# Weight-block sums moved from POOL to DVE in a one-core convolution-and-FFN layer, with padded tile pools and a rewritten last half

## The chip, the cores and the metric

The kernel runs on one core of a Trainium2 chip. The metric is the device time of one execution in microseconds (us), the median over runs. TensorE is called PE, VectorE DVE, ScalarE ACT, GpSimd POOL and SyncE SP. The transfers are issued by SP and ACT.

## What is computed

The reference is one layer on 2048 tokens of width 1024, float32 in and out, batch 1, with depth 1 (so only the convolution mixer and the FFN):

```python
mod = c_act @ ada_w[i] + ada_b[i]
sh_m, sc_m, g_m, sh_f, sc_f, g_f = jnp.split(mod, N_ADA, axis=-1)
h = modulate(rms_norm(x, norm_gains[i, 0]), sh_m, sc_m)
h = short_conv_mixer(h, conv_w_in[j], conv_w[j], conv_w_out[j])
x = x + g_m[:, None, :] * rms_norm(h, norm_gains[i, 1])
h = modulate(rms_norm(x, norm_gains[i, 2]), sh_f, sc_f)
h = swiglu(h, ffn_w_gate_up[i], ffn_w_down[i])
x = x + g_f[:, None, :] * rms_norm(h, norm_gains[i, 3])
```

`short_conv_mixer` is a product to 3 x 1024 features (gate b, gate c, value), a gate, a causal convolution of 3 taps along the tokens, a second gate and a product back to 1024. `swiglu` has an inner width of 2816.

## The kernel before

**Tiling.** Tokens are taken in two units (0 and 1) of 1024, each of two halves of 512. The stages follow each other as in0, out0, in1, out1, gu0, down0, gu1, down1: the product into the mixer, the product out of it, gate and up, down, for each unit. Every stage is done as one level of the Strassen-Winograd scheme: a product of 2 x 2 blocks becomes seven products P1 to P7. Their feature operands are A11, A12, A22 and the sums S1 to S4, their weight operands the blocks 11, 12, 21, 22 and sums of them. Every operand is split in a high part (a cast on ACT) and a low part (a subtraction on DVE), and a product of 4 chunks takes 3 matmuls a chunk: 12 matmuls of 128 x 512 make a slot, the unit of the program's clock.

**Weights.** A group of weights (tiles like `in7b`, `gu11b`: four or five blocks of 128 x 512 in the ring of raw tiles) goes through steps that run a fixed number of slots ahead of its product: loads 9 slots ahead, sums of blocks 7, the high part (ACT, into a tile like `in7P`) 5, the low part (DVE, into the same tile) 4. `Blocks.sum` makes the sums in the stages in and gu: 12 becomes 22-12 ahead of P7 or P6 (called T3), 11+ becomes 12+11 ahead of P6, 21 becomes 21-11+ and 11+ becomes 22-11+ ahead of P5. All four are POOL's, but T3 of the first three groups of in0, which is DVE's. Other sums of weights stay as they are: those of `Between` (`gu0b` to `gu2b`, between the slots of in0 and in1) on DVE, and those that `sums_later` makes for out and down and keeps in DRAM (`out1b`, `down9b`), on POOL. POOL also adds the squares of the norms (`nq`, `out0q`, `down1q`), makes two of the sums of features in `sums`, and the powers of the norms.

**Order.** Every engine executes its instructions in the order in which the program writes them (the helper at L75 records all of them, so all rows of the trace are of that line). An instruction that waits holds up everything behind it on its engine. `Group.after` puts ACT copies of a bank after P1, P6 and P5 and DVE additions after the others; PE goes on adding in the same bank, so a later product waits for the ACT copy.

**The opening.** `start` writes the order of the first three groups of in0 by hand: norms, the modulation, the products of A11, S3, A12 and S2, with `advance("sums", ...)`, `advance("high", ...)` and `advance("low", ...)` between them.

**The end.** In down1 the last half of the tokens has eight tiles of 128 x 512. Each is squared on ACT and added to the sum of squares. `last_half` then takes the mean on PE (`lasts`), 1/sqrt (POOL's power `lastp`, DVE's `lastt` and `lastq`), spreads it on PE (`lastb`, from the diagonal `lastd`), and makes x + gate x norm x z for eight tiles: five on DVE (two instructions each, reading `lastb`), three on POOL (reading `lastr`, an ACT copy of it; their gate is put in before by ACT). `xl` are the tiles of x. The tiles of the half before (`xo`, scaled with `o10r`) are still being written while this runs: one every 2 slots.

Of the kernel before, what the change touches and what calls it, by code (L numbers as in the profile page):

```python
# [10 lines left out]
F32 = mybir.dt.float32  # L11
# [35 lines left out]
def hybrid_conv_layer(  # L47
# [34 lines left out]
    sb = ctx.enter_context(tc.tile_pool(name="sb", bufs=1))  # L82
# [3 lines left out]
    def big(name, dt=F32):  # L86
        return sb.tile([P, 4, CH], dt, tag="big", bufs=NBIG, name=name)

    def raw(name):
        return sb.tile([P, CH], F32, tag="raw", bufs=NRAW, name=name)  # L90

    def pair(name):
        return sb.tile([P, 2, CH], F32, tag="wp", bufs=NWP, name=name)
# [42 lines left out]
    vt = const.tile([P, 112], F32, name="vt")  # L136
# [164 lines left out]
    class Blocks:  # L301
# [194 lines left out]
    class Group:  # L496
# [119 lines left out]
        def ready_z(self, c):  # L616
# [183 lines left out]
    for s in slots:  # L800
# [5 lines left out]
        else:  # L806
            b = of.setdefault((ph.name, s.n), Blocks(ph.kind, s.grp, ph.name == "in0" and s.n < LEAD))
# [68 lines left out]
    def after_down(ph, tok):  # L876
# [10 lines left out]
        yield from spread_later(q, f"o{u}{tok}", partial(put, rb, 0))  # L887
# [16 lines left out]
        for k in range(KD):  # L904
# [6 lines left out]
            yield 2  # L911
# [4 lines left out]
    POOLS = (5, 6, 7)  # L916

    def last_half(ph):

        u, tok = ph.u, 1  # L920
        st = bank("lasts")
        for t in range(4):
            PE.matmul(st[:, t : t + 1], ph.acc[tok][:, t * P : (t + 1) * P], mean, start=True, stop=True)
# [5 lines left out]
        rb = sb.tile([P, CH], F32, tag="rb", bufs=NRB, name="lastr")  # L929
        A.copy(rb, b)  # L930
        mine = [k for k in range(KD) if k not in POOLS]
        for n in range(len(mine)):
            if n < len(POOLS):
                k = POOLS[n]
                z, xt = ph.z(tok, k), ph.xt[k]
                G.tensor_tensor(z, z, rb, ALU.mult)
                G.tensor_tensor(xt, xt, z, ALU.add)
            k = mine[n]
# [4 lines left out]
        for k in POOLS:  # L943
            SP.dma_start(out_tile(u, tok, k), ph.xt[k])
        yield

    def before_last(ph):
# [4 lines left out]
        yield 1  # L952
        for k in POOLS:
            z = ph.z(1, k)
            A.activation(z, z, AF.Copy, scale=col(mG[1], k))
# [271 lines left out]
    schedule(first["down1"] + 73, lambda: run(before_last(phases[-1])))  # L1227
# [85 lines left out]
```

## Time and profile before

| | us |
|---|---|
| median of 3 runs | 2040.47 |
| lowest and highest | 2039.4 and 2041.07 |
| the profiled execution | 2041.43 |
| its span in the trace | 2039.3 |
| PE busy | 1941.7 |
| DVE busy | 1444.0 |
| ACT busy | 855.2 |
| POOL busy | 691.1 |

The time of an execution is 2.1 us longer than the span between the first and the last instruction that the trace shows. Busy time is the sum over instructions of an engine; an engine that is not busy waits or has nothing to do.

### The profile page before, as it was taken

Reading aid. Unit: us, or ns where it says so; the run is one execution under the profiler, and the core shown is the slowest. Engines: PE = TensorE matmul, PEld = TensorE weight load, DVE = VectorE, ACT = ScalarE, POOL = GpSimd, SP = SyncE. Lnnn points to the kernel's source line nnn. Section 1 sums busy time; section 2 is a strip of 40 time slices with the busy share of each in tenths; the row PEclk is TensorE's granted clock in tenths of the full one; section 3 lists DMA queues with packets and bytes.
Section 4 is the critical chain, followed back from the end, with each engine's and each line's share of the span. In section 5 each row is a group of like instructions: output and inputs, shape, how many; then the busy total and the mean of one; then the engine's idle time right before and its main releaser. Section 6 shows DMA issues by size and latency. Waiting matters only on the chain.

```text
span 2039.3 us, 25010 instructions
## 1 busy us (share of the span) xinstructions
PE 1941.7 (95%) x8432; PEld 1578.8 (77%) x8432; DVE 1444.0 (71%) x1878; ACT 855.2 (42%) x1382; POOL 691.1 (34%) x451
## 2 busy tenths in 40 slices
PE   5799998999989899999999999999999999999995
PEld 2578886778767778887888888887888888888884
DVE  4887887886989685699767656667767455465465
ACT  5443355632333663343333445544333333344451
POOL 0324541301542133357856431111443343311022
PEclk9899999999999999999999999999999999999998
DMA  9259959879766875477656788567646234285544
GB/s 382 74 205 352 358 203 327 322 266 347 243 212 206 300 258 175 151 232 257 224 186 218 256 280 308 196 249 258 222 162 220 94 127 132 67 326 208 203 145 136
DMA packets 206193, 463.19 MB, mean 227 GB/s; under 512 B 23024, under 2 KB 38512, under 8 KB 199152
## 3 DMA queue, kind: packets, MB, share of 16 engines
q1 hardware_dynamic: 179136, 397.49, 56.9%
q10 hardware_dynamic: 26928, 64.10, 8.3%
q8 instruction: 66, 1.08, 0.2%
q14 instruction: 63, 0.52, 0.1%
HBM read 328.33 MB, written 133.17 MB: 226 GB/s over the span
## 4 chain that ended last, share of the span: by engine, by line
PE 70%; DVE 13%; DMA 8%; ACT 4%; issue 3%; POOL 1%; SPq 0%; ACTq 0%; DVEq 0%; POOLq 0%
PE gu1P L75 20%; PE gu0P L75 16%; PE down1P L75 10%; PE down0P L75 10%; PE in0P L75 6%; PE in1P L75 5%; PE out1P L75 2%; DMA xx<-xt_d 1%; PE out0P L75 1%; DVE ada L75 1%; DMA xr<-x_d 1%; DVE zz L75 1%; DMA kgu1P<-gu1P 1%; DVE in0y L75 1%; DMA x<-xx 1%
## 5 line engine op out<-in xcount | busy, mean ns | idle before, releaser
L75 DVE TENSOR_TENSOR gu1a<-gu1P,gu1a 128x512 f32<-128x512 f32 x63 | 43.4, 690 | 93.0 <-PE gu1P L75 86.2
L75 DVE TENSOR_TENSOR gu0a<-gu0P,gu0a 128x512 f32<-128x512 f32 x63 | 43.2, 687 | 59.5 <-PE gu0P L75 54.0
L75 POOL TENSOR_TENSOR down0q<-down0q,down0q 128x512 f32<-128x512 f32 x14 | 26.0, 1859 | 152.3 <-ACT down0q L75 152.2
L75 POOL TENSOR_TENSOR down1q<-down1q,down1q 128x512 f32<-128x512 f32 x10 | 16.2, 1618 | 147.0 <-ACT down1q L75 147.0
L75 DVE CUSTOM_DVE_ANT_0 ada<-ada,c 128x512 f32<-128x512 f32 x80 | 62.5, 791 | 0.2 <-ACT c L75 0.2
L75 ACT COPY gu1a<-gu1P 128x512 f32<-128x512 f32 x42 | 24.5, 587 | 89.7 <-PE gu1P L75 78.1
L75 ACT COPY gu0a<-gu0P 128x512 f32<-128x512 f32 x42 | 24.5, 584 | 73.4 <-PE gu0P L75 65.9
L75 ACT COPY gu1g<-gu1P 128x512 f32<-128x512 f32 x24 | 14.1, 588 | 90.7 <-PE gu1P L75 85.9
L75 POOL TENSOR_TENSOR gu1a<-gu1a 128x512 f32<-128x512 f32 x11 | 19.5, 1776 | 89.8 <-DVE gu1g21s L75 24.7
L75 DVE TENSOR_TENSOR gu1g<-gu1P,gu1g 128x512 f32<-128x512 f32 x24 | 16.6, 691 | 44.9 <-ACT gu1g L75 43.6
L75 POOL TENSOR_TENSOR nq<-nq,nq 128x512 f32<-128x512 f32 x28 | 45.7, 1630 | 3.0 <-ACT nq L75 2.8
L75 ACT COPY gu0g<-gu0P 128x512 f32<-128x512 f32 x24 | 14.1, 586 | 72.6 <-PE gu0P L75 72.6
L75 POOL TENSOR_TENSOR out1q<-out1q,out1q 128x512 f32<-128x512 f32 x14 | 24.2, 1726 | 58.5 <-ACT out1q L75 58.4
L75 DVE TENSOR_TENSOR xx<-xx,zz 128x512 f32<-128x512 f32 x32 | 35.9, 1121 | 5.4 <-DMA xx<-xt_d 4.4
L75 DVE TENSOR_TENSOR gu0g<-gu0P,gu0g 128x512 f32<-128x512 f32 x24 | 16.6, 690 | 31.8 <-ACT gu0g L75 31.3
L75 POOL TENSOR_TENSOR out0q<-out0q,out0q 128x512 f32<-128x512 f32 x14 | 24.7, 1764 | 42.4 <-ACT out0q L75 42.3
L75 POOL TENSOR_TENSOR in0b<-in0b,in0b 128x512 f32<-128x512 f32 x7 | 10.7, 1533 | 79.4 <-DVE in1y L75 37.3
L75 POOL TENSOR_TENSOR gu0a<-gu0a 128x512 f32<-128x512 f32 x11 | 19.5, 1777 | 48.3 <-DVE gu0g11s L75 8.0
L75 ACT ACTIVATE gu1a<-gu1a 128x512 f32<-128x512 f32 x42 | 26.5, 633 | 15.0 <-DVE xo L75 7.7
L75 ACT ACTIVATE nq<-xx 128x512 f32<-128x512 f32 x32 | 20.2, 631 | 28.9 <-DVE xx L75 24.7
L75 ACT ACTIVATE gu0a<-gu0a 128x512 f32<-128x512 f32 x42 | 26.6, 633 | 13.5 <-DVE gu0a L75 12.2
L75 DVE TENSOR_TENSOR down2P<-down2P,down2P 128x512 fp32r<-128x512 f32 x14 | 11.1, 795 | 28.6 <-ACT down2P L75 28.6
(3209 smaller groups left out, 7014.8 us busy)
## 6 DMA issues: line engine op xcount, KB each, us to landing
ada<-ada_d SPq DMA_DIRECT2D x64, 256.0 KB, 5.2
act0A<-gu0a SPq DMA_DIRECT2D x33, 256.0 KB, 4.1
act1A<-gu1a SPq DMA_DIRECT2D x33, 256.0 KB, 3.2
ada<-ada_d SPq DMA_DIRECT2D x16, 512.0 KB, 8.9
zz<-z SPq DMA_DIRECT2D x32, 256.0 KB, 4.2
xx<-xt_d SPq DMA_DIRECT2D x32, 256.0 KB, 4.4
x<-xx ACTq DMA_DIRECT2D x32, 256.0 KB, 3.9
down0S<-act0S SPq DMA_DIRECT2D x8, 1024.0 KB, 7.4
```

The costliest lines, as they stand in the source:

```text
L75: return tc.keep_in_program_order(f(*args, **kwargs))
```

## The change

It has three parts.

**Sums.** All sums of `Blocks.sum` are DVE's now: 221 instructions of 128 x 512 leave POOL's list and stand in DVE's, at the place in the program where they stood (69 in the stages in0 and in1, 152 in gu0 for the groups gu3 to gu21; the groups are summed once and kept or held).

**Pools.** The tiles of `big`, `pair` and `raw` get tile pools of their own, and the constants are padded by 24 floats a partition, so that these tiles start at multiples of 512 bytes in a partition; before, `big` and `raw` started 320 bytes and `pair` 64 bytes past such a multiple.

**End.** All eight tiles of the last half get their gate from ACT ahead of time. The last tile's square stays apart (`lastq` on ACT) and has four matmuls of its own into `lasts`, and one DVE addition of four columns. For five tiles PE adds x and the scaled z in a bank (`lastx`, a matmul with the identity each), ACT copies the bank and issues the store; for three DVE multiplies and adds and SP stores. `lastr` and POOL's part are gone. The half before is spread after 2 slots, not 4, and written every 1.5 slots.

```diff
-                E = V if self.kind == "in" and self.opening else G
-                E.tensor_tensor(b["12"], b["22"], b["12"], ALU.subtract)
+                V.tensor_tensor(b["12"], b["22"], b["12"], ALU.subtract)
             if op == "P6":
-                G.tensor_tensor(b["11+"], b["12"], b["11+"], ALU.add)
+                V.tensor_tensor(b["11+"], b["12"], b["11+"], ALU.add)
             if op == "P5":
-                G.tensor_tensor(b["21"], b["21"], b["11+"], ALU.subtract)
-                G.tensor_tensor(b["11+"], b["22"], b["11+"], ALU.subtract)
+                V.tensor_tensor(b["21"], b["21"], b["11+"], ALU.subtract)
+                V.tensor_tensor(b["11+"], b["22"], b["11+"], ALU.subtract)
...
-    sb = ctx.enter_context(tc.tile_pool(name="sb", bufs=1))
+    bigs, pairs, raws, sb = (ctx.enter_context(tc.tile_pool(name=n, bufs=1)) for n in ("bigs", "pairs", "raws", "sb"))
...
-    vt = const.tile([P, 112], F32, name="vt")
+    vt = const.tile([P, 112 + 24], F32, name="vt")[:, :112]
...
-            add_square(ph.acc, tok, z, f"{ph.name}q{tok}{n}", V if ph.last and c == "21" else G, 0.5 if ph.last else 1)
             ph.tiles_done[tok] += 1
+            scaled_z = partial(A.activation, z, z, AF.Copy, scale=col(mG[1], n))
+            if ph.last and ph.tiles_done[1] == KD:
+                ph.sq = tmp("lastq")
+                A.activation(ph.sq[:, :CH], z, AF.Square)
+                scaled_z()
+            else:
+                add_square(ph.acc, tok, z, f"{ph.name}q{tok}{n}", V if ph.last and c == "21" else G, 0.5 if ph.last else 1)
+                if ph.last and tok:
+                    later(1, scaled_z)
...
-        yield from spread_later(q, f"o{u}{tok}", partial(put, rb, 0))
+        yield from spread_later(q, f"o{u}{tok}", partial(put, rb, 0), 2 if ph.last else 4)
...
-            yield 2
+            yield 1.5 if ph.last else 2
...
+        for k in ON_PE[:2]:
+            add_x(k)
+        for i, sq in enumerate((ph.acc[tok], ph.sq)):
+            for t in range(4):
+                PE.matmul(col(st, 4 * i + t), sq[:, t * P : (t + 1) * P], mean, start=True, stop=True)
+        for k in ON_PE[2:]:
+            add_x(k)
         v = small(4, "lastv")
         V.tensor_scalar(v, st[:, :4], EPS, None, ALU.add)
+        V.tensor_tensor(v, v, st[:, 4:8], ALU.add)
         dg = diagonal(at_once(root(v, "last")), "last")
         b = bank("lastb")
         PE.matmul(b, one, dg[:, :CH], start=True, stop=True)
...
+        for k in ON_PE + tuple(k for k in range(KD) if k not in ON_PE):
             z, xt = ph.z(tok, k), ph.xt[k]
-            V.scalar_tensor_tensor(z, z, col(mG[1], k), b, ALU.mult, ALU.mult)
-            V.tensor_tensor(xt, xt, z, ALU.add)
-            SP.dma_start(out_tile(u, tok, k), xt)
+            V.tensor_tensor(z, z, b, ALU.mult)
+            if k in ON_PE:
+                PE.matmul(sums[k], ident, z, start=False, stop=True, skip_group_check=True)
+                A.copy(xt, sums[k])
+                A.dma_start(out_tile(u, tok, k), xt)
+            else:
+                V.tensor_tensor(xt, xt, z, ALU.add)
+                SP.dma_start(out_tile(u, tok, k), xt)
```

DVE's order in the opening, at the end of the S2 products, before (`in0P`, `in1P`, `in2P` are the low parts of the weights of the first three groups, `in0S1l` the low part of the features S1):

```order
L75 TENSOR_TENSOR in0b_11_456<-in0P_2_567,in0b_11_456 128x512
L75 TENSOR_TENSOR in0P_590<-in0b_462,in0P_590 128x512
L75 TENSOR_TENSOR in1P_595<-in1b_465,in1P_595 128x512
L75 TENSOR_TENSOR in0c<-in0c,in0d 128x2048
L75 TENSOR_TENSOR in2P_600<-in2b_468,in2P_600 128x512
```

DVE's order at the same place now:

```order
L75 TENSOR_TENSOR in0b_11_465<-in0P_2_576,in0b_11_465 128x512
L75 TENSOR_TENSOR in0b_201<-in0b_201,in0b_471 128x512
L75 TENSOR_TENSOR in0b_471<-in0b_180,in0b_471 128x512
L75 TENSOR_TENSOR in0P_599<-in0b_471,in0P_599 128x512
L75 TENSOR_TENSOR in1b_203<-in1b_203,in1b_474 128x512
L75 TENSOR_TENSOR in1b_474<-in1b_184,in1b_474 128x512
L75 TENSOR_TENSOR in1P_604<-in1b_474,in1P_604 128x512
L75 TENSOR_TENSOR in2b_205<-in2b_205,in2b_477 128x512
L75 TENSOR_TENSOR in2b_477<-in2b_188,in2b_477 128x512
L75 TENSOR_TENSOR in0c<-in0c,in0d 128x2048
L75 TENSOR_TENSOR in2P_609<-in2b_477,in2P_609 128x512
```

Six sums stand between the last S2 work and the low parts of P5; POOL made them beside the S2 low parts.

DVE's order in the middle of in0, where the sums of the group `in7` come, before (`in0b_21` and `in0y` are outputs of the group that is finished there):

```order
L75 TENSOR_TENSOR in7P_1404<-in7b_1297,in7P_1404 128x512
L75 TENSOR_TENSOR in7P_1425<-in7b_1322,in7P_1425 128x512
L75 TENSOR_TENSOR in6P_1449<-in6b_1200,in6P_1449 128x512
L75 TENSOR_TENSOR in0b_21_1271<-in0P_5_1282,in0b_21_1271 128x512
L75 TENSOR_TENSOR in0y_1074<-in0b_21_1271,in0y_1074 128x512
```

DVE's order at the same place now:

```order
L75 TENSOR_TENSOR in7P_1413<-in7b_1306,in7P_1413 128x512
L75 TENSOR_TENSOR in7b_1382<-in7b_1384,in7b_1382 128x512
L75 TENSOR_TENSOR in7b_1386<-in7b_1382,in7b_1386 128x512
L75 TENSOR_TENSOR in7P_1434<-in7b_1331,in7P_1434 128x512
L75 TENSOR_TENSOR in6P_1458<-in6b_1209,in6P_1458 128x512
L75 TENSOR_TENSOR in0b_21_1280<-in0P_5_1291,in0b_21_1280 128x512
L75 TENSOR_TENSOR in0y_1083<-in0b_21_1280,in0y_1083 128x512
```

The two sums read blocks that come by DMA; the low parts and the output of the group before now stand behind that wait.

PE's order at the very end, before:

```order
L75 MATMUL down1P_3_15639<-down1A_15709,down11P_15959 128x512
L75 MATMUL lasts<-mean,down1q_15761 128x1 x4
L75 MATMUL lastb<-lastd,one 128x512
```

And now:

```order
L75 MATMUL down1P_3_15648<-down1A_15718,down11P_15984 128x512
L75 MATMUL lastx_16071<-xl_15836,ident 128x512
L75 MATMUL lastx_16073<-xl_15838,ident 128x512
L75 MATMUL lasts<-mean,down1q_15778 128x1 x4
L75 MATMUL lasts<-mean,lastq 128x1 x4
L75 MATMUL lastx_16083<-xl_15840,ident 128x512
L75 MATMUL lastx_16085<-xl_15842,ident 128x512
L75 MATMUL lastx_16087<-xl_15828,ident 128x512
L75 MATMUL lastb<-lastd,one 128x512
L75 MATMUL lastx_16071<-down1z_15303,ident 128x512
```

Ten matmuls with the identity are added, five ahead of `lastb` and five behind it (the first of them shown).

## Rows read from the trace of the kernel before

**Rows 1.** The head of the page: the span, and busy time of each engine, its share of the span and its instructions.

```profile
span 2039.3 us, 25010 instructions
PE 1941.7 (95%) x8432; PEld 1578.8 (77%) x8432; DVE 1444.0 (71%) x1878; ACT 855.2 (42%) x1382; POOL 691.1 (34%) x451
```

**Rows 2.** Stretches of the span: its start and end, its length, then busy time and instructions of PE, the weight loads, DVE, ACT and POOL, the granted clock, the DMA share and GB/s.

```profile
56.00:64.00 8.00, 8.00 (x35) 4.30 (x34) 7.93 (x12) 0.83 (x3) 6.28 (x4) 0.98 0.41 118
81.00:101.00 20.00, 15.22 (x57) 11.22 (x56) 18.62 (x16) 7.11 (x11) 12.62 (x7) 0.91 0.14 40
100.00:300.00 200.00, 194.81 (x847) 159.49 (x846) 166.23 (x216) 80.30 (x144) 87.87 (x58) 0.99 0.79 285
500.00:700.00 200.00, 180.12 (x761) 144.89 (x760) 174.48 (x252) 82.51 (x145) 76.95 (x49) 0.96 0.74 246
1100.00:1300.00 200.00, 200.00 (x884) 165.58 (x884) 123.73 (x148) 87.95 (x129) 58.86 (x38) 1.00 0.74 258
```

**Rows 3.** What PE waited for in three stretches, 60 to 140, 500 to 700 and 900 to 1100 us: engine and line, what released it, us in total, times, the longest.

```profile
PE in0P L75 <- DVE in0S2l L75: 4.2, 3, 2.4
PE in0P L75 <- ACT in0c L75: 2.7, 1, 2.7
PE in0P L75 <- DVE mB L75: 2.4, 1, 2.4
...
PE in1P L75 <- ACT in1c L75: 6.9, 2, 5.7
...
PE gu0P L75 <- ACT gu0a L75: 1.4, 1, 1.4
```

**Rows 4.** Groups of POOL and DVE by operation and tile: busy time, mean ns of one, then the idle time ahead of them and what ended it. The first two are of the whole span, the last two of 1100 to 1300 us.

```profile
L75 POOL TENSOR_TENSOR gu17b<-gu17b,gu17b 128x512 f32<-128x512 f32 x8 | 11.5, 1432 | 21.5 <-DVE gu17P L75 11.8 <-issue 6.5 <-DVE gu0a L75 1.3
L75 POOL TENSOR_TENSOR in10b<-in10b,in10b 128x512 f32<-128x512 f32 x8 | 11.8, 1481 | 22.1 <-DMA in10b<-w_in_d 18.2 <-DVE in10P L75 3.8
L75 DVE TENSOR_TENSOR gu20P<-gu20b,gu20P 128x512 fp32r<-128x512 f32 x7 | 8.3, 1200 | 1.4 <-ACT gu20P L75 1.4
L75 DVE TENSOR_TENSOR down0P<-down0P,down0P 128x512 fp32r<-128x512 f32 x5 | 3.4, 683 | 0.0
```

**Rows 5.** The timeline of DVE and POOL in the opening: start, us, engine, line, operation, count.

```profile
57.14 1.75 DVE L75 TENSOR_TENSOR in1P<-in1b,in1P 128x512 fp32r<-128x512 f32 x1
60.49 1.24 DVE L75 TENSOR_TENSOR mf<-ms,ms 128x2 f32<-128x2 f32 x1
...
56.67 1.67 POOL L75 TENSOR_TENSOR in0b<-in0b,in0b 128x512 f32<-128x512 f32 x1 [22.06 <-DVE ms L75]
...
82.31 1.78 DVE L75 TENSOR_TENSOR in1P<-in1b,in1P 128x512 fp32r<-128x512 f32 x1
...
87.39 3.44 DVE L75 TENSOR_TENSOR in0S2l<-in0a,in0S2h 128x512 fp32r<-128x512 f32 x2
90.75 0.68 DVE L75 TENSOR_TENSOR in0b<-in0P,in0b 128x512 f32<-128x512 f32 x1
91.35 0.68 DVE L75 TENSOR_TENSOR in0P<-in0b,in0P 128x512 fp32r<-128x512 f32 x1
...
125.65 3.52 DVE L75 SCALAR_TENSOR_TENSOR in0y<-in0c,vt,in0y 128x512 f32<-128x512 f32 x2
```

**Rows 6.** The timeline at late loads: POOL and DVE near `in7b`, the ACT cast behind them, POOL at `in2b`, POOL at `gu11b`, and PE at its longest wait in in1. In brackets the idle time before and what ended it.

```profile
190.52 1.28 DVE L75 TENSOR_TENSOR in7P<-in7b,in7P 128x512 fp32r<-128x512 f32 x2
...
195.58 1.29 POOL L75 TENSOR_TENSOR in7b<-in7b,in7b 128x512 f32<-128x512 f32 x1 [8.54 <-DMA in7b<-w_in_d]
...
200.05 0.62 ACT L75 CAST in7P<-in7b 128x512 fp32r<-128x512 f32 x1 [6.36 <-POOL in7b L75]
...
548.77 1.29 DVE L75 TENSOR_TENSOR in2P<-in2b,in2P 128x512 fp32r<-128x512 f32 x2
...
552.00 2.64 POOL L75 TENSOR_TENSOR in2b<-in2b,in2b 128x512 f32<-128x512 f32 x2 [6.35 <-DMA in2b<-w_in_d]
...
952.67 2.66 POOL L75 TENSOR_TENSOR gu11b<-gu11b,gu11b 128x512 f32<-128x512 f32 x2 [6.84 <-DMA gu11b<-w_gu_d]
...
593.31 1.22 PE L75 MATMUL in1P<-in1S2h,in9P 128*128 128x512 f32 x2 [5.67 <-ACT in1c L75]
598.60 0.83 PE L75 MATMUL in1P<-in1S3h,in9P 128*128 128x512 f32 x2
```

**Rows 7.** The timeline of the end, and a group by tile (`o10b`, a spread like `lastb`: duration of one matmul at its least, median and most in ns).

```profile
2014.95 0.39 PE L75 MATMUL down1P<-down1A,down11P 128*128 128x512 f32 x1
2017.51 1.05 PE L75 MATMUL lasts<-mean,down1q 128*128 128x1 f32 x8 [2.17 <-DVE down1q L75]
2021.56 2.07 PE L75 MATMUL lastb<-lastd,one 128*128 128x512 f32 x2 [3.00 <-DVE lastd L75]
...
2024.29 0.75 DVE L75 SCALAR_TENSOR_TENSOR down1z<-down1z,mG,lastb 128x512 f32<-128x512 f32 x1 [2.78 <-ACT lastr L75]
...
2034.54 0.69 DVE L75 TENSOR_TENSOR xo<-xo,down1z 128x512 f32<-128x512 f32 x1
...
2016.10 0.63 ACT L75 ACTIVATE down1q<-down1z 128x512 f32<-128x512 f32 x1 [6.79 <-DVE down1z L75]
...
L75 PE MATMUL o10b<-o10d,one x2: 590/590/591, 1978.2 to 1978.7; 128*128 128x512 f32 x2
```

More of the change, by code (lines that the diff above doesn't have):

```diff
@@ L86, in big @@
     def big(name, dt=F32):
-        return sb.tile([P, 4, CH], dt, tag="big", bufs=NBIG, name=name)
+        return bigs.tile([P, 4, CH], dt, tag="big", bufs=NBIG, name=name)
     def raw(name):
-        return sb.tile([P, CH], F32, tag="raw", bufs=NRAW, name=name)
+        return raws.tile([P, CH], F32, tag="raw", bufs=NRAW, name=name)
     def pair(name):
-        return sb.tile([P, 2, CH], F32, tag="wp", bufs=NWP, name=name)
+        return pairs.tile([P, 2, CH], F32, tag="wp", bufs=NWP, name=name)
     def tmp(name):
@@ L242, in spread, with spread_later @@
         return rb
-    def spread_later(q, name, put):
+    def spread_later(q, name, put, lag=4):
         dg = diagonal(q, name)
-        yield 4
+        yield lag
         put(spread(dg, name))
@@ L306, in hybrid_conv_layer, with __init__ @@
         FROM = {"11": 0, "12": 1, "22": 2, "21": 3, "11+": 0}
-        def __init__(self, kind, grp, opening=False):
+        def __init__(self, kind, grp):
             self.kind, self.grp, self.b, self.split, self.summed = kind, grp, {}, {}, set()
-            self.opening = opening
         def load(self, op):
@@ L806, in hybrid_conv_layer @@
         else:
-            b = of.setdefault((ph.name, s.n), Blocks(ph.kind, s.grp, ph.name == "in0" and s.n < LEAD))
+            b = of.setdefault((ph.name, s.n), Blocks(ph.kind, s.grp))
             w = Weight(ph.kind, s.grp, s.op, b, ph.name == "in0" and s.g.i in (1, 2))
@@ L910, in after_down, with add_x @@
             later(1, partial(A.dma_start, out_tile(u, tok, k), xt))
-            yield 2
+            yield 1.5 if ph.last else 2
     def out_tile(u, tok, k):
         return out[u * 2 + tok, k // 4][:, (k % 4) * CH : (k % 4 + 1) * CH]
-    POOLS = (5, 6, 7)
+    ON_PE = (4, 5, 6, 7, 0)
     def last_half(ph):
         u, tok = ph.u, 1
+        sums = {}
+        def add_x(k):
+            sums[k] = bank(f"lastx{k}")
+            PE.matmul(sums[k], ident, ph.xt[k], start=True, stop=False, skip_group_check=True)
         st = bank("lasts")
-        for t in range(4):
-            PE.matmul(st[:, t : t + 1], ph.acc[tok][:, t * P : (t + 1) * P], mean, start=True, stop=True)
+        for k in ON_PE[:2]:
[5 more added lines that the diff above has]
+            add_x(k)
         v = small(4, "lastv")
         V.tensor_scalar(v, st[:, :4], EPS, None, ALU.add)
+        V.tensor_tensor(v, v, st[:, 4:8], ALU.add)
         dg = diagonal(at_once(root(v, "last")), "last")
@@ L928, in last_half @@
         PE.matmul(b, one, dg[:, :CH], start=True, stop=True)
[L929 to L938, printed above, removed]
-            z, xt = ph.z(tok, k), ph.xt[k]
-            V.scalar_tensor_tensor(z, z, col(mG[1], k), b, ALU.mult, ALU.mult)
-            V.tensor_tensor(xt, xt, z, ALU.add)
-            SP.dma_start(out_tile(u, tok, k), xt)
-        for k in POOLS:
-            SP.dma_start(out_tile(u, tok, k), ph.xt[k])
+        for k in ON_PE + tuple(k for k in range(KD) if k not in ON_PE):
+            z, xt = ph.z(tok, k), ph.xt[k]
+            V.tensor_tensor(z, z, b, ALU.mult)
[6 more added lines that the diff above has]
+                SP.dma_start(out_tile(u, tok, k), xt)
         yield
@@ L951, in before_last @@
             SP.dma_start(ph.xt[k], x1_d[ph.u][1][:, k, :])
[L952 to L955, printed above, removed]
     for ph in phases:
@@ L1226, in hybrid_conv_layer @@
     schedule(first["down0"] + 22, lambda: run(mods_later((5,), 2)))
-    schedule(first["down1"] + 73, lambda: run(before_last(phases[-1])))
+    schedule(first["down1"] + 73, lambda: before_last(phases[-1]))
     def multiply(s, ks=None, follow=True):
```

## The prediction

> **What bounds the kernel now.** I read the head of the page first: PE is busy for 95% of the span and DVE for 71%, POOL for 34% [rows 1]. A change that frees POOL and loads DVE can therefore only act where PE is not busy. The stretches show where that is: from 1100 to 1300 us PE is busy for all of it, and a change in DVE's work there is worth nothing; from 500 to 700 us it misses 19.9 us, in the opening 81 to 101 us 4.8 of 20 [rows 2]. In the opening DVE is full (7.93 of 8 us, 18.62 of 20) while POOL works beside it, and PE's waits there end with DVE: the low parts of S2 4.2 us in three waits, `mB` 2.4, a copy 2.7 that comes through ACT [rows 2, 3]. In in1 the waits end with ACT, the longest 5.7 us [rows 3]. In gu0 they are small (1.4) [rows 3]. The last place is the end, where nothing is left to overlap: the last full matmul starts at 2014.95 and the span ends at 2039.3, 24.4 us later [rows 1, 7].
>
> **DVE against POOL.** The row that prices the first part of the change is a DVE subtraction of 128x512 with both inputs in SBUF: 0.68 us when POOL is idle, with the next one 0.60 behind it, and 1.75 to 1.78 while a POOL sum runs [rows 5]. Even an addition of two columns (`mf`) took 1.24 beside POOL [rows 5]. In the middle of gu0 the low parts of a group whose sums POOL makes meanwhile (`gu20P`) took 1.20 on the mean, those of one that has none (`down0P`) 0.68 [rows 4]. Now 221 sums cost DVE 221 x 0.605 = 134 us more, and POOL, at 1.43 each [rows 4], 316 us less. What DVE gets back lies between nothing and 221 x 1.1 = 243 us (if each sum lengthened one DVE instruction by 1.78 - 0.68). I take half, 122 us, since seven low parts of `gu20P` were on the mean 0.52 longer and DVE is not always at a two-input instruction. So DVE's net load is about +12 us, between -109 and +134, and where DVE is full the sign depends on how closely the two met.
>
> The Trainium skill has the rule for this ("SBUF — State Buffer", section "Who interferes with whom"): a DVE instruction with two SBUF inputs contends with a GpSimd instruction that reads SBUF, through a pair of ports that is an exclusive lock. It speaks for the change where POOL's sums vanish and against it in one respect: each moved sum is itself such an instruction, so it meets the squares and kept sums that POOL retains. By that rule a sum that meets one costs up to 1.78 like the rows above, and 221 sums of which POOL's remaining share (691 - 316 = 375 of 2039 us, 18%) hits one in five would add 221 x 0.18 x 1.1 = 44 us of DVE, most of it in stages in which PE is full; the sum of this forecast leaves that out.
>
> **The opening (to 134 us): -4.** From 57.14 on, two low parts and the two `mf` run beside POOL; the two low parts take 3.35 us to 60.49 instead of 1.2, and each `mf` 1.1 us too long: 4.3 us. Three sums go in, 1.8. From 82.31 to 90.75 five low parts take 8.44 us instead of 5 x 0.60 = 3.0: 5.4 us back, and PE's waits for S2 (4.2 us [rows 3]) are exactly there. Behind them the six sums stand ahead of the low parts of P5, 6 x 0.605 = 3.6, so that of the 5.4 only 1.8 is left for S1. Near 125.65 two instructions took 3.52 instead of 1.3 [rows 5], against which four sums take 2.4: nothing. On the way to the copies PE can be earlier by 2.5 + 1.8 = 4.3; I take 4. The bounds are 1 (half of the excess was in the shadow of PE's other waits, and the sums cost in full) and 7 (PE goes by the S2 work alone, which gains 2.5 + 5.4 = 7.9, less a sum or two).
>
> **in0 and in1: 0 and -1.** Here DVE is 83% to 87% busy (166.2 and 174.5 of 200 us [rows 2]), and it now waits itself for the blocks. What stands behind a sum on DVE is low parts, additions that empty PE's banks and the tails of finished groups; ACT's casts stand behind those, and PE behind ACT's copies. Before, POOL took the waits: 18.2 us at `in10b` [rows 4], 8.54 at `in7b`, and ACT already stood behind POOL for 6.36 us there [rows 6]. So that chain (load, sum, cast, copy, PE) does not get a new member; it swaps one, and the sum in it becomes 1.29 - 0.68 = 0.6 us shorter. DVE reached the place of `in7b` at about 191.2 and the block came at 195.5, a wait of some 4.3 us; at `in2b` 550.0 and 552.0, 2 us [rows 6]. PE has two slots of 2.72 us (12 matmuls; 884 records in 200 us are 0.226 each [rows 2]) between a product and the next use of its bank, 5.4 us, which covers either. I take 0 for in0 and out0 (bounds -2 and +2) and -1 for in1 and out1, where PE waits most (bounds -6 and +5: below, the longest wait of 5.7 us goes; above, one late load adds its 4.3).
>
> **gu0 and after: -1.** The waits of 900 to 1100 us (1.4 and less [rows 3]) come from ACT behind POOL's load wait (`gu11b`, 6.84 us [rows 6]); some of it may stay, so -1, between -3 and 0. From 1100 us on PE is full; 0.
>
> **The pools: 0.** No row shows an operation whose time depends on where in a partition a tile starts: `gu20P` and `down0P`, `xo` and `down1z` lie in different rings, and two SBUF inputs cost 0.68 to 0.69 in each [rows 4, 5, 7]. The price is 0, with the rival below.
>
> **The end: -5.** Before: last matmul 2014.95, its bank is added, squared (2016.10, 0.63), added on DVE, `lasts` from 2017.51 for 1.05, the root and the diagonal until 2021.51, `lastb` 2021.56 to 2023.63 at the low clock (1.03 a pass; `o10b`, after full work, 0.59, with the second pass 0.5 behind the first [rows 7]), then `lastr` and DVE from 2024.29 to 2035.23; the span ends 4.07 us after that. Now the DVE addition of the last square (0.7) and its handover go, but two `lastx` (4 passes x 0.5 to 0.59 = 2.0 to 2.4 from 2015.3) and eight more passes of `lasts` (1.05) stand before the root: `lasts` ends at 2018.4 to 2019.5 where it ended at 2018.56; I take 2018.8. Then 3.0 us as before and 0.2 for the added columns: 2022.0. Three `lastx` keep PE busy meanwhile, so `lastb` is two passes of 0.59: 2023.2. DVE then has 11 instructions (eight products, three additions) 0.61 apart with no POOL beside it: 2029.9. PE's branch: the fifth z at about 2026.3, five pairs of passes of 1.0 to 1.18 from 2023.9, a copy of 0.59: 2029.5 to 2030.4. With the same 4.07 us behind: 2033.6 to 2034.5. Eight stores of 256 KB now fall in some 6 us instead of 10, so I give a part back: -5, between -7 and -3.
>
> **Sum.** -4 + 0 - 1 - 1 - 5 = -11 on the profiled execution of 2041.43, so 2030.4. That execution was 0.96 us above the median of 2040.47; against the median the forecast is 2029.5.
>
> **Rivals.**
>
> *The opening is given back.* Between 100 and 300 us the DMA share is 0.79 [rows 2]; loads that come as fast as before meet a PE that is 4 us earlier. For: POOL's waits for loads [rows 4, 6]. Against: PE lost 5.2 us only in that stretch, so its slack was rarely used up. Only the end and gu0 count: 2040.5 - 6 = 2034.5.
>
> *Late loads stop DVE (slower).* The listing by tile has a dozen groups in in0, in1 and gu0 at which POOL waited for a load. If DVE stands 2 to 4.3 us at each, some 30 us, and what it holds up is banks that PE needs, then a wait decides from 5.4 us on, after two of them come in one stretch. With half of it reaching PE, 15 us, and after it the lower clock (following the 5.67 us wait 12 matmuls took 598.60 - 593.31 = 5.3 us instead of 2.72 [rows 6], 2.6 more), the time is 2040.5 - 10 + 17.6 = 2048. For: DVE's load in these stages. Against: it already waits in the same places for its own inputs.
>
> *The end runs at the low clock.* With ten added matmuls of two passes at 1.03 instead of 0.59, PE's branch alone takes 5 x 2.07 = 10.4 us behind `lastb`: z from 2024.6 on gives 2035.6, a copy and the store 2040.3, so the end gains nothing: 2040.5 - 6 + 1 = 2035.5. For: the clock did fall here. Against: it fell after PE had idled, and now PE has little idle time.
>
> *Alignment speeds the transfers.* If every transfer took a tenth less (a choice; no row prices it), the first 56 us before 57.14, in which DVE and PE wait for loads, would shrink by some 6 us and the later waits for blocks by 2: 2029.5 - 8 = 2021.5. No row shows it, since no tile of these starts at a multiple of 512 bytes now. The Trainium skill ("DMA: Bandwidth & Descriptors", section "How a descriptor splits into AXI transactions") has it that a descriptor which does not start at a multiple of 256 bytes takes an extra transaction; for a 2 KB row that is nine for eight, and no run here shows whether it holds for the tile's side.
>
> **How the numbers follow.** Forecast 0.62, given back 0.14, late loads 0.13, low clock 0.06, alignment 0.05. The bounds of the forecast's terms, put together and not all at one end, are -20 and -3: 2020.5 to 2037.5. The range reaches on to part of the late loads: 2020 to 2042. About 0.2% (4.1 us) is what a measurement of this kernel can tell from no change: faster means below 2036.4. The forecast gives 0.57 of its 0.62 there, alignment 0.05, given back 0.10, low clock 0.03: faster 0.75. The same takes the rest of these, 0.12, and some of the late loads: 0.14. Slower 0.11.
>
> **What would show it.** Right: POOL has some 230 instructions and 370 us, DVE about as much busy time as before, within 30 us; five low parts in 3 us instead of 8.4 at the S2 products; PE at the product of 133 us four earlier; DVE's last instruction near 2030 in a clock that stays high. Wrong: DVE rows with a load as releaser of over 5 us and PE waiting for ACT copies behind them in in0 or in1; transfers of blocks that land faster; `lastx` passes of a microsecond.

## The result, and the profile after

The changed kernel takes 2028.55 us (median of 4 runs, 2027.0 to 2029.27) against 2040.77 us: a ratio of 0.9935, with a 95% interval of 0.9923 to 0.9947, so 12 to 13 us less. The forecast was 2029.5 us. The profiled execution took 2029.04 us.

The head of its page, to be read beside [rows 1]:

```profile
span 2027.3 us, 24977 instructions
PE 1947.9 (96%) x8460; PEld 1582.1 (78%) x8460; DVE 1463.0 (72%) x2100; ACT 864.1 (43%) x1391; POOL 346.0 (17%) x224
```

POOL lost 345 us. DVE has 222 instructions more and is busy for only 19 us more. The sums cost more than that, as two groups of them show (count, busy time, mean ns of one):

```profile
L75 DVE TENSOR_TENSOR gu16b<-gu16b,gu16b 128x512 f32<-128x512 f32 x8 | 8.7, 1085 | 0.1
L75 DVE TENSOR_TENSOR in10b<-in10b,in10b 128x512 f32<-128x512 f32 x8 | 5.5, 690 | 2.4 <-DMA in10b<-w_in_d 2.2
```

Most groups take 0.69 us a sum, but in eleven groups of gu and in `in4b` the mean is 0.81 to 1.08, since some sums run beside work that POOL kept. Added up over all groups, the 224 sums on DVE (three were there before) last 181 us, 27 of them above 0.69 each. So DVE got back some 140 to 160 us that it had spent beside POOL (an estimate: 19 us net, against 160 us if sums follow each other as closely as before, 0.605 apart, or 179 by their durations).

The same stretches as in [rows 2] (start and end, length, busy time and instructions of PE, the weight loads, DVE, ACT and POOL, the granted clock, the DMA share, GB/s):

```profile
56.00:64.00 8.00, 7.13 (x32) 4.18 (x29) 6.76 (x15) 2.23 (x4) 0.00 (x0) 1.00 0.29 100
81.00:101.00 20.00, 13.67 (x50) 10.37 (x49) 16.60 (x19) 7.79 (x11) 0.00 (x0) 0.84 0.17 53
100.00:300.00 200.00, 196.34 (x860) 161.28 (x859) 164.88 (x254) 84.33 (x151) 34.09 (x23) 1.00 0.77 284
500.00:700.00 200.00, 184.21 (x779) 147.74 (x778) 172.98 (x280) 86.54 (x148) 37.58 (x24) 0.97 0.74 254
```

In the opening POOL does nothing. From 100 to 300 us DVE executes 38 instructions more in 1.4 us less. The timeline of DVE and PE in the opening, at the places of [rows 5] (start, us, engine, line, operation, count, in brackets the idle time before and what ended it), and last the stretch of 95 to 101 us:

```profile
54.78 3.61 PE L75 MATMUL pms<-ada,cact 128*1 128x256 f32 x16
...
57.99 0.68 DVE L75 TENSOR_TENSOR in1P<-in1b,in1P 128x512 fp32r<-128x512 f32 x1
59.19 0.15 DVE L75 TENSOR_TENSOR mf<-ms,ms 128x2 f32<-128x2 f32 x1
...
80.14 0.69 DVE L75 TENSOR_TENSOR in1P<-in1b,in1P 128x512 fp32r<-128x512 f32 x1
81.94 1.29 DVE L75 TENSOR_TENSOR in0S2l<-in0a,in0S2h 128x512 fp32r<-128x512 f32 x2
83.75 1.41 DVE L75 TENSOR_TENSOR in0b<-in0b,in0b 128x512 f32<-128x512 f32 x2
85.90 0.69 DVE L75 TENSOR_TENSOR in0P<-in0b,in0P 128x512 fp32r<-128x512 f32 x1 [0.74 <-ACT in0P L75]
...
89.28 1.41 DVE L75 TENSOR_TENSOR in2b<-in2b,in2b 128x512 f32<-128x512 f32 x2
90.61 2.29 DVE L75 TENSOR_TENSOR in0c<-in0c,in0d 128x2048 f32<-128x2048 f32 x1
...
95.36 1.22 PE L75 MATMUL in0P<-in0S1h,in0P 128*128 128x512 f32 x2 [5.71 <-ACT in0c L75]
107.03 0.61 PE L75 MATMUL in0P<-in0S4h,in0P 128*128 128x512 f32 x2
...
133.51 0.61 PE L75 MATMUL in0P<-in0S3h,in3P 128*128 128x512 f32 x2
...
95.00:101.00 6.00, 5.02 (x11) 3.54 (x12) 5.55 (x4) 3.85 (x7) 0.00 (x0) 0.50 0.20 71
```

The low part that took 1.78 us takes 0.69, the addition of two columns 0.15 instead of 1.24. The five low parts up to 83.15 follow each other at 0.60. PE's three waits for the S2 low parts [rows 3] are gone. Behind them stand the six sums, three pairs of 1.41 us, the first two followed by a wait of 0.74 us for ACT's cast; they turn into one wait of PE of 5.71 us before S1, and after it the granted clock is 0.50, the lower of its two levels (1.2 GHz). At 133.51 PE is 4.2 us ahead: the same matmul stood at 137.72 before, as these rows of the kernel before show.

```profile
56.52 3.61 PE L75 MATMUL pms<-ada,cact 128*1 128x256 f32 x16
107.17 0.61 PE L75 MATMUL in0P<-in0S4h,in0P 128*128 128x512 f32 x2
95.00:101.00 6.00, 5.38 (x24) 4.13 (x23) 4.62 (x4) 4.79 (x7) 4.52 (x2) 1.00 0.18 47
137.72 0.63 PE L75 MATMUL in0P<-in0S3h,in3P 128*128 128x512 f32 x1
331.94 0.79 PE L75 MATMUL out0P<-out0S20h,out0P 128*128 128x512 f32 x1 [4.96 <-ACT out0P L75]
679.27 0.80 PE L75 MATMUL out1P<-out1S20h,out0P 128*128 128x512 f32 x1 [4.10 <-ACT out0P L75]
```

Two things in these rows limit the 4.2 us. PE was already 1.7 us ahead at 55 us (54.78 against 56.52), before any moved sum had run; so the opening itself, from there to 133 us, became 2.5 us shorter (78.7 instead of 81.2). And the lead did not come at S1: the last product of S2 starts 8.6 us earlier (89.27 instead of 97.86), but after the wait and the slow clock the first product of S4 is only 0.1 earlier (107.03 instead of 107.17).

The last two rows are landmarks (the first matmul of its kind) in out0 and out1; the next fence has the same ones of the changed kernel.

```profile
328.09 0.80 PE L75 MATMUL out0P<-out0S20h,out0P 128*128 128x512 f32 x1 [5.21 <-ACT out0P L75]
671.85 0.79 PE L75 MATMUL out1P<-out1S20h,out0P 128*128 128x512 f32 x1 [3.00 <-ACT out0P L75]
2007.12 0.40 PE L75 MATMUL down1P<-down1A,down11P 128*128 128x512 f32 x1
```

So PE is 3.9 us ahead in out0, 7.4 in out1, and 7.8 at the last full matmul (2014.95 before [rows 7]). From there to the end of the span are 20.2 us instead of 24.4: 4.2 more, 12.0 in all.

What DVE waited for between 100 and 1100 us, the largest rows with a load as releaser (engine and line, releaser, us in total, times, the longest):

```profile
DVE in7b L75 <- DMA in7b<-w_in_d: 7.5, 2, 5.0
DVE in9b L75 <- DMA in9b<-w_in_d: 7.0, 3, 3.5
...
DVE gu11b L75 <- DMA gu11b<-w_gu_d: 5.6, 2, 4.7
```

With the smaller ones of this view these waits are some 35 us (9 before). The rival of late loads had their size right (some 30 us). In the table of PE's waits no row of these stages grew by more than 2 us.

The end (timeline, as [rows 7]):

```profile
2007.35 1.88 PE L75 MATMUL lastx<-xl,ident 128*128 128x512 f32 x4
2009.07 0.95 PE L75 MATMUL lasts<-mean,down1q 128*128 128x1 f32 x8
2009.88 1.03 PE L75 MATMUL lasts<-mean,lastq 128*128 128x1 f32 x8
2010.77 2.82 PE L75 MATMUL lastx<-xl,ident 128*128 128x512 f32 x6
2013.95 1.12 PE L75 MATMUL lastb<-lastd,one 128*128 128x512 f32 x2 [0.36 <-DVE lastd L75]
2015.86 4.56 PE L75 MATMUL lastx<-down1z,ident 128*128 128x512 f32 x10 [0.78 <-DVE down1z L75]
...
2015.12 3.68 DVE L75 TENSOR_TENSOR down1z<-down1z,lastb 128x512 f32<-128x512 f32 x6 [1.22 <-PE lastb L75]
2021.48 0.69 DVE L75 TENSOR_TENSOR xl<-xl,down1z 128x512 f32<-128x512 f32 x1
```

The spread `lastb` takes 1.12 us instead of 2.07; PE now idles only 0.36 us before it, where it idled 3.00. DVE's eleven instructions end 7.05 us after they begin (2015.12 to 2022.17), and the span ends 5.1 us after that, where 4.07 were assumed.

### The profile page after: what moved, and what is told of

Its sections match the earlier page's. It is cut to its first block, busy times and chain, and to the rows that moved or that the text cites. A ratio compares the mean times of both kernels' runs of the same rounds, so it can differ in the third digit from the quotient of the medians.

```text
span 2027.3 us, 24977 instructions
## 1 busy us (share of the span) xinstructions
PE 1947.9 (96%) x8460; PEld 1582.1 (78%) x8460; DVE 1463.0 (72%) x2100; ACT 864.1 (43%) x1391; POOL 346.0 (17%) x224
## 3 DMA queue, kind: packets, MB, share of 16 engines
q8 instruction: 66, 1.08, 0.2%
## 4 chain that ended last, share of the span: by engine, by line
PE 74%; DVE 10%; DMA 8%; issue 4%; ACT 4%; ACTq 0%; POOL 0%; SPq 0%; POOLq 0%; DVEq 0%
PE gu1P L75 20%; PE gu0P L75 18%; PE down0P L75 10%; PE down1P L75 9%; PE in1P L75 7%; PE in0P L75 7%; PE out1P L75 2%; DMA xr<-x_d 1%; DMA x<-xx 1%; PE out0P L75 1%; DVE zz L75 1%; DVE in0y L75 0%; DVE ada L75 0%; DMA in0a<-xt_d 0%; DVE xx L75 0%
## 5 line engine op out<-in xcount | busy, mean ns | idle before, releaser
L75 POOL TENSOR_TENSOR in0y<-in0y 128x512 f32<-128x512 f32 x4 | 5.7, 1434 | 153.5 <-DVE in0b0s L75 98.8
L75 ACT ACTIVATE nq<-xx 128x512 f32<-128x512 f32 x32 | 20.2, 630 | 22.4 <-DVE xx L75 21.4
L75 DVE TENSOR_TENSOR xx<-xx,zz 128x512 f32<-128x512 f32 x32 | 27.0, 845 | 1.1
```

The lines of the kernel that those rows point to most:

```text
L75: return tc.keep_in_program_order(f(*args, **kwargs))
```

## The experiments

Twelve kernels ran. The **theory** was that the gain has two parts that add up: DVE's time beside POOL, which two-input instructions of both engines cost each other, and the end. The **rivals**: the tiles' places in a partition; the sum's shorter way; late loads; and that an early opening is given back.

**The three parts, one at a time.** The first run changes only the pools:

```diff
-    sb = ctx.enter_context(tc.tile_pool(name="sb", bufs=1))
+    bigs, pairs, raws, sb = (ctx.enter_context(tc.tile_pool(name=n, bufs=1)) for n in ("bigs", "pairs", "raws", "sb"))
...
-    vt = const.tile([P, 112], F32, name="vt")
+    vt = const.tile([P, 112 + 24], F32, name="vt")[:, :112]
```

> The kernel before with the pools and the padding alone: big, pair and raw tiles start at multiples of 512 bytes, all sums and the end as before. Theory (the tiles' place costs nothing): 2040.5 us, within 2, and PE reaches the products of S2 in the opening (91.5 us for in1) as before. Rival (alignment speeds the transfers or PE): PE's first products of the opening come 1 to 2 us earlier, as they do in the changed kernel before any sum has moved (54.8 against 56.5 us), and the time is 2039 or less; if it were more than the opening, 2033.

Measured: 2041.34 us, ratio 1.0002 (0.9991 to 1.0013). The tiles' places cost and bring nothing that can be measured, and PE's first products come no earlier than before (S2 of `in1` at 92.6 us, 91.5 before). The lead of 1.7 us at 55 us that the profile of the changed kernel shows is not the pools' work: here the product of 54.78 stands at 57.77, and in the profile of the end alone, which has the order of before up to down1, at 54.29. It differs that much from one profile to the next.

The second takes the end alone, the third the sums alone:

> The kernel before with the rewritten end alone, sums on POOL and one pool. Theory (the parts add): the last full matmul of down1 within 0.5 us of where it was (2014.95), the end 4.6 to 5 us shorter, 2035.5 us. Rival (the shorter end needs the free POOL or an earlier start): less than 3 us shorter, 2038 or more.

> The kernel before with all 221 sums on DVE and nothing else. Theory (DVE gets back its time where POOL worked beside it): about 4 us in the opening and 3 in in1, 2033 us, with DVE busy some 1465 us in all. Rival (late loads, now waited for by DVE): DVE waits for blocks of over 30 us in all and PE loses by them in in0 and in1, 2040 or more.

The end alone: 2036.94 us, 0.9976 (0.9967 to 0.9985), 4.9 us less; its last full matmul stands at 2015.08 (2014.95 before), and the span ends 20.2 us behind it, as in the changed kernel. The sums alone (the edit is the first block of the diff above): 2033.43 us, 0.9962 (0.9949 to 0.9976), 7.8 us less, with DVE busy for 1463.0 us. Together 12.7 us, against 13.3 by the ratio of the changed kernel: the parts add, as far as the intervals can tell.

**POOL made busy again.** In the next three DVE's order is the changed kernel's, and POOL gets work that nobody needs. First, after each sum, an addition that reads the finished sum:

```diff
+    idle = const.tile([P, 384], mybir.dt.bfloat16, name="idle")
+
+    def spent(t):
+        G.tensor_tensor(idle, t[:, :384], t[:, :384], ALU.add)
...
                 V.tensor_tensor(b["12"], b["22"], b["12"], ALU.subtract)
+                spent(b["12"])
```

> The changed kernel, and after each sum POOL makes an instruction nobody needs: it adds a finished sum of 128x384 to itself into a tile of its own (221 of them, about 1.1 us each). DVE's order is that of the changed kernel. Theory (the gain comes from POOL's silence: the ports are free): DVE's instructions beside POOL go to 1.7 us again, DVE is busy 80 us or more longer, and the opening and in1 lose what they had won and more: 2036 to 2046 us. Rival (the gain comes from the sum's shorter way, 0.7 us on DVE instead of 1.3 to 1.7 on POOL, and from its place in order): stays at 2028.5, within 2.

Measured: 2066.61 us, 1.0121 (1.0107 to 1.0135), 38 us above the changed kernel and beyond the range expected. Its head:

```profile
PE 1961.6 (95%) x8460; PEld 1591.2 (77%) x8460; DVE 1525.1 (74%) x2100; ACT 862.4 (42%) x1391; POOL 616.7 (30%) x448
```

DVE's 2100 instructions take 62 us more. But POOL also holds blocks here until it has read them, and its other work stands behind these waits, so that the run alone doesn't settle the cause. The next two touch no block: two additions of a small tile to itself for each sum, or four memsets of it.

```diff
+    idle = const.tile([P, 200], F32, name="idle")
...
     def spent(t):
+        G.tensor_tensor(idle, idle, idle, ALU.add)
+        G.tensor_tensor(idle, idle, idle, ALU.add)
...
+        for _ in range(4):
+            G.memset(idle, 0.0)
```

(The first two lines of the body are the one run, the loop is the other. Both also call it behind each sum, as above.)

> The changed kernel, and with each sum POOL makes two additions of 128x200 of a small tile to itself, which nobody waits for and which wait for nobody (442 of them, no block is touched). Theory (POOL's reads of SBUF slow DVE): DVE's instructions beside them lengthen, DVE is busy 40 to 100 us more, 2032 to 2050 us. Rival (in the run with additions on finished sums the time came from blocks that POOL held, so that loads came late): 2028.5, within 2.

> The same with four memsets of the small tile instead of the two additions: POOL writes SBUF as often but reads nothing. Theory (it is the second input of DVE that meets POOL's reads): DVE's instructions keep their times, 2028.5 within 2. Rival (any work of POOL slows DVE): as the run with additions, in proportion to POOL's busy time.

The additions: 2047.5 us, 1.0035 (1.0022 to 1.0048), 19 us above the changed kernel. The memsets: 2026.06 us, 0.9927 (0.9914 to 0.994), not to be told from the changed kernel. The head of the page and POOL's group of the useless work (busy time, mean ns of one, then the idle time before), with the additions:

```profile
PE 1954.5 (96%) x8460; PEld 1583.0 (77%) x8460; DVE 1532.5 (75%) x2100; ACT 863.8 (42%) x1391; POOL 696.1 (34%) x673
...
L75 POOL TENSOR_TENSOR idle<-idle 128x200 f32<-128x200 f32 x448 | 345.2, 771 | 29.3
```

and with the memsets:

```profile
PE 1948.5 (96%) x8460; PEld 1584.0 (78%) x8460; DVE 1453.3 (72%) x2100; ACT 862.6 (43%) x1391; POOL 584.1 (29%) x1121
...
L75 POOL MEMSET idle<- 128x200 f32 x897 | 239.1, 267 | 47.4 <-POOLq L1326 0.3
```

345 us of POOL that reads cost DVE 69.5 us and the kernel 19; 239 us of POOL that only writes cost nothing (DVE is busy 9.7 us less). If any work of POOL slowed DVE, the memsets would by proportion have cost DVE some 48 us (an estimate, 69.5 x 239 / 345). That decides for POOL's reads: DVE's order, the sums' way and the blocks are the same in both.

The Trainium skill ("SBUF — State Buffer", section "Who interferes with whom") states that a DVE instruction with two SBUF inputs contends with a GpSimd instruction that reads SBUF, "not with one that only writes it". These two runs agree (69.5 us of DVE against none).

**Which sums bring it.** `E` is made an argument of the group, G or V by stage:

```diff
-    b = of.setdefault((ph.name, s.n), Blocks(ph.kind, s.grp))
+    b = of.setdefault((ph.name, s.n), Blocks(ph.kind, s.grp, G if ph.kind == "gu" else V))
```

> The changed kernel with the 152 sums of gu0 and gu1 back on POOL; those of in0 and in1 stay on DVE, the pools and the end as changed. Theory (PE is full there, so only the stretch near 950 us counts): 0 to 2 us slower than the changed kernel, 2028.5 to 2030.5. Rival (DVE's net load in gu matters): 4 us or more slower or faster.

> The changed kernel with the sums of the first three groups of in0 alone on DVE; the rest of in0, in1 and gu back on POOL. Theory (each stage keeps its own share): the opening's 4 us and the end's 5 stay, in1's 3 us and gu0's 1 go: 2032 to 2033. Rival A (what the opening wins is only worth as much as the later stages let it be, since their loads set the pace): 2035 to 2036, the end alone. Rival B (the opening does it all): 2028.5.

> The changed kernel with the 69 - 24 sums of in0 on DVE (all groups) and those of in1 and gu on POOL again. Theory (the opening's gain needs the rest of in0 to follow, in1 has its own): the stages to out0 as in the changed kernel (3 to 4 us ahead of before at the first product of in1), in1 as before: 2031 to 2032. Rival (loads set the pace of in0, whoever makes the sums): like the run with the opening alone, 2035 to 2036.

With the sums of gu on POOL: 2029.67 us, 0.9946 (0.9928 to 0.9964), within what was expected; 152 of the 221 sums are worth 1 to 2 us, which the intervals don't separate from nothing. With the opening's alone on DVE: 2035.89 us, 0.9973 (0.9964 to 0.9982), no better than the end alone (0.9976). With all of in0 on DVE: 2029.15 us, 0.9953 (0.9941 to 0.9966); 2 us better than expected by the median, as expected by the ratio (0.9953 of 2040.77 is 2031.2).

The first theory (each stage keeps its own share) fell with the second of these. In its trace PE stands at the product of 133 us at 135.09, 2.6 us ahead of before, and then:

```profile
135.09 0.62 PE L75 MATMUL in0P<-in0S3h,in3P 128*128 128x512 f32 x2
257.13 0.79 PE L75 MATMUL in0P<-in0S1h,in9P 128*128 128x512 f32 x1 [2.65 <-ACT in0c L75]
...
255.88 0.63 ACT L75 ACTIVATE xr<-xr 128x512 f32<-128x512 f32 x1 [8.48 <-DMA xr<-x_d]
...
256.51 0.57 ACT L75 COPY in0c<-in0P 128x512 f32<-128x512 f32 x1
```

At 257.13 it is 0.7 us behind the kernel before (256.44), and at the landmark of out0 4.4 behind (336.30). ACT waited 8.48 us for a load of x, and the copy that PE needs stood behind it. So the lead met a load that came no earlier. SP issued its loads of x here at 249.50 and 250.57, as in the kernel before (249.37 and 251.27), behind three loads of `in10b` in its order; in the changed kernel it did so at 244.98 and 246.54. In the run with all of in0's sums on DVE that matmul stood at 251.28, with no wait ahead of it: the lead is kept when the middle of in0 gets along too. What in that middle lets SP come to these loads earlier was not tried by itself.

**The clock at the end.** All matmuls of x behind the spread:

```diff
-        for k in ON_PE[:2]:
-            add_x(k)
...
         PE.matmul(b, one, dg[:, :CH], start=True, stop=True)
+        for k in ON_PE:
+            add_x(k)
```

> The changed kernel with all five matmuls of x with the identity moved behind the spread of the last norm, so that PE idles while DVE and POOL make the root. Theory (these matmuls keep PE's clock up, as the rival of the low clock had it): the spread takes 2.0 us again instead of 1.12, each pass after it a microsecond for some time, the clock of the end shows 0.50, and the span after the last full matmul grows by 3 to 6 us: 2032 to 2034. Rival (PE's clock does not fall, or PE's branch has room): within 2 of 2028.5, since the root starts 1.7 us earlier.

Measured: 2031.94 us, 0.996 (0.9945 to 0.9975), 3.4 us above the changed kernel by the medians, with intervals that just overlap. PE's timeline there:

```profile
2013.15 1.05 PE L75 MATMUL lasts<-mean,lastq 128*128 128x1 f32 x8 [0.66 <-ACT lastq L75]
2017.24 2.07 PE L75 MATMUL lastb<-lastd,one 128*128 128x512 f32 x2 [3.04 <-DVE lastd L75]
2019.11 5.69 PE L75 MATMUL lastx<-xl,ident 128*128 128x512 f32 x10
2024.64 4.46 PE L75 MATMUL lastx<-down1z,ident 128*128 128x512 f32 x10
```

and stretches of it:

```profile
2015.00:2018.00 3.00, 0.76 (x1) 0.50 (x2) 1.36 (x7) 0.00 (x0) 0.69 (x1) 0.50 0.00 0
2018.00:2022.00 4.00, 4.00 (x6) 1.54 (x5) 2.64 (x5) 0.00 (x0) 0.00 (x0) 0.55 0.00 0
2022.00:2025.00 3.00, 3.00 (x8) 1.33 (x7) 2.93 (x6) 0.00 (x0) 0.00 (x0) 1.00 0.12 48
```

After an idle time of 3.04 us the spread takes 2.07 us at the lower level (0.50), and the clock is back by 2022. From the last full matmul (2011.31) to the end of the span (2034.7) are 23.4 us, 3.2 more than in the changed kernel. Not all of that is the clock. `lasts` ends 0.9 us sooner after the last full matmul here, and that pays for the longer spread (0.95), so DVE begins at the same distance (8.05 us, 8.00 in the changed kernel). What comes later is PE's branch: the ten passes of x now stand between the spread and the z, and take 5.69 us instead of 1.88 + 2.82. So the early matmuls of x do two things: they put work into the wait for the root, and they keep the clock. By these rows the clock is some 2 us of PE's time (0.95 + 1.0, an estimate); its share of the 3.2 was not separated.

**Further along the same way.** The additions of squares of out and of the norm after it, and the sums of features of in, go to DVE too:

```diff
-                add_square(ph.acc, tok, z, f"{ph.name}q{tok}{n}", V if ph.last and c == "21" else G, 0.5 if ph.last else 1)
+                add_square(ph.acc, tok, z, f"{ph.name}q{tok}{n}", V if ph.last and c == "21" or ph.kind == "out" else G, 0.5 if ph.last else 1)
...
-        G.tensor_tensor(t[:, 1, :], t[:, 0, :], t[:, 1, :], ALU.subtract)
+        E = V if d is not act_d[0] and d is not act_d[1] else G
+        E.tensor_tensor(t[:, 1, :], t[:, 0, :], t[:, 1, :], ALU.subtract)
...
-            later(2, partial(add_square, acc, 0, xt, f"nq{u}{tok}{k}"))
+            later(2, partial(add_square, acc, 0, xt, f"nq{u}{tok}{k}", V))
```

> The changed kernel with more of POOL's work on DVE: the additions of squares of the out stages and of the norm after them, and the two sums of features of each stored tile in in0 and in1 (some 70 instructions of 128x512); POOL keeps the sums of weights for out and down, the squares of down, the sums in gu and the powers. Theory (each POOL instruction beside DVE costs it more than making it would): DVE busy about the same, another 1 to 4 us off, in in1 above all: 2025 to 2028. Rival (DVE now waits in order for ACT's squares, which come late): 2030 or more.

Measured: 2016.42 us, 0.9886 (0.9871 to 0.99), 12 us less than the changed kernel by the medians, 10 by the ratios, where 1 to 4 were expected. Head and landmark, from an execution of 2013.09 us:

```profile
PE 1944.9 (97%) x8460; PEld 1583.5 (79%) x8460; DVE 1445.3 (72%) x2172; ACT 864.0 (43%) x1391; POOL 231.0 (11%) x152
...
659.88 0.50 PE L75 MATMUL out1P<-out1S20h,out0P 128*128 128x512 f32 x1 [2.00 <-ACT out0P L75]
```

DVE executes 72 instructions more and is busy 18 us less; PE is 12 us earlier in out1, 10.7 of which it gains behind the landmark of out0. On the mean, each of these POOL instructions had cost DVE more than making it does.

The last run adds two moves of order to this: the kept squares' matmuls ahead of the first matmul of x, and S1's sum and cast ahead of the opening's six sums.

```diff
-        for k in ON_PE[:2]:
-            add_x(k)
...
-        for k in ON_PE[2:]:
-            add_x(k)
+            for k in (ON_PE[:1], ON_PE[1:])[i]:
+                add_x(k)
...
+        f.s1()
+        f.high("S1")
```

> The kernel with the squares on DVE, and two moves of order. At the end the four matmuls of the kept sums of squares stand ahead of the first matmul of x, and the four of the last square behind it, so that the root can start 0.9 us earlier while PE stays busy. In the opening the sum of the features S1 (2.29 us on DVE) and its cast stand ahead of the six sums of weights, so that PE's wait for the S1 products (over 4 us near 95 us) starts to end earlier. Theory: 0.9 us at the end; in the opening 1 to 2 us at 95 us, of which nothing need be left at the end of in0, since loads set the pace there: 2014.5 to 2016, not to be told from 2016.4. Rival (the opening counts): 5 us less, 2011.

Measured: 2015.82 us, 0.9873 (0.9856 to 0.9889), not to be told from the run before. PE's products of S1 start at 95.72 instead of 96.66, and nothing is left of it at the landmark of out0 (327.26, 326.80 in the run before). PE's wait there ends with ACT's copy `in0c`, and in this run that copy stands behind the cast of `in2P`, which waits for the last of the six sums. The end is 0.7 us shorter by the trace. The run beats the kernel before and the changed one by the interval, but neither move was run alone, and none is shown to be worth anything in time.

## Why the prediction was right, step by step

**DVE against POOL** was right in mechanism: the additions against the memsets show that it is POOL's reads. The net load was right too (12 us forecast, 19 measured), but partly by luck, since both of its terms were too small: the sums were priced at 134 us and took some 160 to 180, and 122 us were to come back where some 140 to 160 did. One reason is a term that the sum left out, sums that meet the work that POOL kept: 25 of the 224 took over 1 us, each of them beside a POOL addition or subtraction, and 27 us in all lie above 0.69 each. For this the Trainium skill ("SBUF — State Buffer", section "Who interferes with whom") has the rule on two-input DVE instructions and POOL's reads, from which the forecast had worked out 44 us beside its sum; the trace agrees, with 27.

**The opening, -4**, agrees with the lead at 133 us (4.2) by luck. 1.7 of it was there at 55 us, by chance between two profiles; from 55 to 133 us the gain is 2.5 in this pair, and nothing between the two profiles that reach the product of 54.78 latest (57.77 with the pools alone, 57.90 with the sums of gu on POOL; 79.5 us from there in both). The way was wrong as well: S2 ended 8.6 us earlier, 6.9 of it won since 55 us (up to 7.9 were worked out), but the wait before S1 (5.71 us, with two waits for ACT's casts between the sums) and the low clock behind it, which the sum had at nothing, took all of it by S4; what is left at 133 us was won behind that. And its reading as a share of its own was wrong: with these sums alone the kernel gains nothing over the end alone. The step that failed there is that the lead was worth its size in time. The first rival (given back) described that run; in the changed kernel the 36 other sums of in0, forecast at 0, are what keeps the lead.

**in0 and out0, 0**: PE's lead went from 4.2 to 3.9 us. **in1 and out1, -1**: the lead grew by 3.5 in the profiled pair, so this term was too small. That the sums of in1 are the reason is likely but not shown: in the run with these on POOL the lead grew by 2.3 as well (from 6.0 at the landmark of out0 to 8.3 at that of out1). From one landmark to the other, five profiles with these sums on POOL (the kernel before, the pools, the end, the opening alone, in0 alone) take 344.4 to 347.7 us, mean 346.2, and five with them on DVE (the changed kernel, the sums alone, gu on POOL, the memsets, the late matmuls of x) 340.9 to 345.4, mean 343.1. In time there is the difference between 0.9953 and 0.9935, whose intervals overlap.

**gu and after, -1**: 0.4 in the profile, 1 to 2 by the run with gu on POOL, neither clear of zero.

**The end, -5**: 4.2 in the profile and, alone, 4.9 by time (3.1 to 6.7 by its interval). In all profiles the new end takes 20.2 us, within 0.3, from the last full matmul (but for the two runs that reorder it), the old one 24.4 to 24.8. The terms: `lasts` ended 3.8 us after the start of the last full matmul (2010.91 - 2007.12), forecast 3.85; `lastb` took 1.12, forecast 1.18; DVE's eleven 7.05, forecast 6.7; the stores behind it 5.1 instead of 4.07. That last term was the one mis-sized, as the part given back allowed for.

**The pools, 0**: shown. **The sum:** in the profiled pair 12.0 us are 1.7 before 55 us, 2.5 in the opening, -0.3 in in0 and out0, 3.5 in in1 and out1, 0.4 in gu and after, and 4.2 at the end; the forecast had 4, 0, 1, 1 and 5. So the total is right, and the mechanism of the sums and of the end, but the division among the stages is luck where it agrees. **The rivals:** DVE waited for loads as the second had it, some 35 us, without PE losing by it; that POOL's waits had stood in the same chain, as the forecast argued, was not tested by itself. The low clock did not come at the end, and in the run that lets PE idle there the end is 3.2 us longer, in part by the clock. Alignment had nothing to it that can be measured.

## What to carry to other kernels

Price work on POOL by what it does to DVE: in this kernel an instruction of 128x512 that reads SBUF on POOL beside DVE's two-input work cost DVE about as much as making it (the 221 sums a little less, the 72 instructions of the squares run more), so where DVE is the engine that others wait for, moving such work onto DVE can relieve it. A lead won early is only worth what the stretch behind it can keep; try a part by itself before putting a figure on it. Compare a lead with where the two profiles stood before the change could act. At the end of a kernel, put useful matmuls into the wait for a reduction: they shorten what follows twice, by their own work and by the clock (3.2 us together here).

## What was not expected of the hardware

Moving 72 more instructions from POOL to DVE made DVE's busy time 18 us shorter, not about the same. POOL's writes without reads left DVE's times alone at 239 us of POOL work, while reads at 345 us cost DVE 69.5 us (this was the theory, and it held). Even an addition of two columns took as long as the rest of a POOL sum: 1.24 us, to 61.73, where the sum that ran beside it ended at 61.71 (0.15 without). A start of tiles at multiples of 512 bytes, instead of 64 or 320 bytes past one, changed no time (1.0002).
